# Doubled key tiles written by VectorE and turned a step later, and the gate's partial rows added instead of selected: one step of a hybrid attention layer

## The chip, the core and the metric

The kernel runs on one core of one Trainium2 chip. The metric is the time of one execution in microseconds (us), as the device measures it. Engines are named as in the profile: PE is TensorE, DVE is VectorE, ACT is ScalarE, POOL is GpSimd, SP is the sync engine, which only issues transfers here. ACT issues transfers too; "ACTq" and "SPq" rows are such issues.

## The reference

One layer of a diffusion backbone: 128 prompt tokens and 1024 latent tokens, width 1024. Cut to what matters:

```
shift, scale, gate = split(silu(cond) @ w_mod + b_mod, 3)      # cond: c (latent) and c_ctx (prompt)
h = rmsnorm(x, norm_gain) * (1 + scale) + shift
q_a, k_a, v_a, g_a, q_b, k_b, v_b, g_b = split(h @ w_in)       # 8 query heads and 2 key heads of 64 columns, per branch
q, k = rmsnorm per head, with gains; latent tokens: axial rotary positions
o_a = attention(q_a, all latent keys + 128 cached keys)        # prompt tokens: prompt keys only
o_b = attention(q_b, keys within 128 positions + cached keys, a learned sink per head)
y = x + gate * (concat(o_a * silu(g_a), o_b * silu(g_b)) @ w_out)
```

The outputs are y for prompt and latent tokens, and the prompt's keys and values. All in float32. The gate is one row of 1024 numbers per condition (two rows in all).

## The kernel before, in words

Tokens are worked in nine tiles of 128 (tile 0 is the prompt, tiles 1 to 8 are latent). To keep float32 accuracy at the fast matmul rate, each operand is split into a rounded high part (a cast, mostly on ACT) and a low part (the difference, on DVE or POOL), and a product is made of three: high x high, high x low, low x high. A projection of one tile is thus 24 products of 128x128x512 (lines 244 to 248).

**What sets the order.** The order is written by hand. `block` (line 265) runs one projection in two halves of 12 products; ahead of each half it calls `tick`, which moves a step counter on by one and runs what was entered in the `agenda` for that step with `later(n, f)`, in the order of entry. So a "step" is a half block of TensorE work, and side work is interleaved with it. At the end every engine is held to this program order; only waits between engines are left to the hardware. Buffers of one tag rotate: a tile that takes a buffer waits until the last reader of its predecessor is done.

The stages, in order: modulation and normalisation; gate projection of branch A; query projection of branch A, then of branch B (tiles 1 to 8, then 0); key and value projection (tile 0, then 1 to 8); gate projection of branch B; attention with the output projection.

**Queries** (`query`, line 614). For each tile: squares (ACT) and their sums (DVE), the power on POOL (`rsqrt_mean`, line 166), scaling and rotation (DVE), then at its seventh step the turn: four transposes by PE into a PSUM bank (line 650), the high part copied by ACT (653) and stored at once, the low part made by DVE a step later (658) and, with `later(1, ...)`, stored a step after that (`put`, two issues of 128 KB each on ACT's queue, line 663). `qo0` and `qo1` have two buffers each. The turns alternate between the two PSUM banks D and E (`bank_tr`, line 147), and so does everything else that calls `bank_tr`.

**The gate row** (`gate_rows`, line 597). During the queries of branch B, ahead of tile 4 and of tile 8, PE makes one half of the gate rows each time: eight products with 32 stationary columns, spread over the four column groups of the array, so that a PSUM bank holds four partial sums for each of the two conditions, at partitions 0-1, 32-33, 64-65 and 96-97. A step later ACT copies the bank to `grow` (604); three steps later `gate_sum` (591) adds the four partials by a float32 product with the selecting matrix `sel` (593), into a bank from `bank_tr`, and DVE adds the bias (594) and SP stores the row. Behind the second one come the splits of the key and value weights (231, 233), in the last query block.

**Keys** (`key`, line 783). The first three tiles (`AHEAD`), 0, 1 and 2, are projected while the query stage still drains; their key work is then entered at consecutive steps, the others' at every second step. For each tile: squares at its step 1; scaling and rotation on DVE at step 3; at step 4 (`final`, 813) DVE adds the two rotary products into `kf` (816; a copy for the prompt, 818) and in the same step ACT writes `k2`, each key head's 64 columns twice (`twice`, 749); at step 6 PE turns `k2` by four transposes into bank D or E (755), ACT casts the high parts (759 to 771), and a step later DVE makes the low parts (773), which lets the bank go. The cached keys (`put_keys(kc, ...)`, 831) go the same way from step 8. `kh`, the tag of `k2`, has two buffers.

Of the kernel before, what the change touches and what calls it, by code (L numbers as in the profile page):

```python
# [9 lines left out]
F32 = mybir.dt.float32  # L10
# [3 lines left out]
ALU = mybir.AluOpType  # L14
# [4 lines left out]
P = 128  # L19
# [32 lines left out]

WO_STEPS = ((0, 4, 4), (1, 5, 5), (2, 6), (3, 7), (4, 8, 6), (5, 9), (6, 11), (7, 12, 10), (8, 13), (9, 14), (10, 16))
TURN = 2
QUERY_AT = (0, 2, 3, 6)
PAD = 2
SECOND_FROM = 5
# [18 lines left out]
VC_AT = 6  # L76
ONES_AT = 14
KEY_AT = (1, 3, 4)
AHEAD = 3


# [24 lines left out]
def hybrid_step(ctx, tc, x_prompt, x_sample, cache_k_a, cache_v_a, cache_k_b, cache_v_b,  # L106
# [17 lines left out]
    def later(n, f):  # L124

        agenda.setdefault(now[0] + n, []).append(f)
# [20 lines left out]
    def bank_tr(name):  # L147
        turn["tr"] += 1
        return bank("DE"[turn["tr"] % 2], name)
# [159 lines left out]
    with tc.tile_pool(name="st", bufs=2, side="right") as st:  # L309
# [9 lines left out]
        def group_sum(out, eye):  # L319
            nc.vector.tensor_tensor(out, eye[:, 0:2], eye[:, 32:34], op=ALU.add)  # L320
            for a in (64, 96):
                nc.vector.tensor_tensor(out, out, eye[:, a : a + 2], op=ALU.add)

        wm = []

# [253 lines left out]
    with tc.tile_pool(name="qt", bufs=2, side="right") as qt:  # L579
# [4 lines left out]
        sil32 = qt.tile([P, KT, 32], F32, name="sil32g", bufs=1)  # L584
        nc.gpsimd.memset(sil32, 0.0)
        nc.vector.tensor_copy(sil32[:, :, 0:2], silc.rearrange("p (c k) -> p k c", c=2))
        sel = qt.tile([P, 2], F32, name="selg", bufs=1)
        group_sum(sel, ident_r.bitcast(F32))
        wg, bg = [], []

        def gate_sum(n, grow):
            pgs = bank_tr(f"pgs{n}")
            nc.tensor.matmul(pgs[0:2], sel, grow, start=True, stop=True)
            nc.vector.tensor_tensor(bg[n], pgs[0:2], bg[n], op=ALU.add)
            nc.sync.dma_start(gate_row[:, 512 * n : 512 * n + 512], bg[n])

        def gate_rows(n):
            pg = bank_mm(f"pgate{n}")
            for k in range(KT):
                a = 32 * (k % 4)  # L600
                nc.tensor.matmul(pg[a : a + 32], sil32[:, k, :], wg[2 * n + k // 4][:, k % 4, :],
                                 start=(k < 4), stop=(k >= 4), tile_position=(0, a))
            grow = qt.tile([P, 512], F32, tag="grow", name=f"grow{n}", bufs=1)
            later(1, lambda: nc.scalar.copy(grow, pg))
            later(3, lambda: gate_sum(n, grow))

        def load_wg(i):
            n, b = divmod(i, 2)
# [5 lines left out]
        def query(pq, m, t, tabs, n=1):  # L614

            nm = f"q{m}_{t}"
            pqv = pq.rearrange("p (h d) -> p h d", d=HD)
            v = {}

            def squares():  # L620
                sq = qt.tile([P, 8, HD], F32, tag="sq", name=f"sq{nm}")
                nc.scalar.activation(sq, pqv, AF.Square)  # L622
                ss = qt.tile([P, 8], F32, tag="ss", name=f"ss{nm}")
                nc.vector.tensor_reduce(ss, sq, axis=AX.X, op=ALU.add)
                v["r"] = rsqrt_mean(qt, ss, HD, 8, nm)

            def scale():
                qn = qt.tile([P, 8, HD], F32, tag="qn", name=f"qn{nm}")
                nc.vector.tensor_tensor(qn, pqv, v["r"].unsqueeze(2).to_broadcast([P, 8, HD]), op=ALU.mult)
                v["qn"] = qn  # L630
                if t:
                    v["rot"] = rope_products(qt, qn, 8, *tabs[m], t, nm)

            def rotated():

                qf = qt.tile([P, 4, 2, HD], F32, tag="qf", name=f"qf{nm}", bufs=3)
                out = qf.rearrange("p h g d -> p g h d")
                pair = lambda a: a.rearrange("p (g h) d -> p g h d", g=2)
                if t:
                    nc.vector.tensor_tensor(out, *(pair(a) for a in v["rot"]), op=ALU.add)  # L640
                else:
                    nc.vector.tensor_tensor(
                        out, pair(v["qn"]), gain4[:, 2 * m, :].unsqueeze(1).unsqueeze(1).to_broadcast([P, 2, 4, HD]),
                        op=ALU.mult)
                v["qf"] = qf

            def turned():
                ptq = bank_tr(f"pt{nm}")
                for h in range(4):
                    nc.tensor.transpose(ptq[:, P * h : P * h + P], v["qf"][:, h].rearrange("p g d -> p (g d)"),  # L650
                                        ident_r.bitcast(F32))
                qo = [qt.tile([P, 512], F32R, tag=f"qo{i}", name=f"qo{i}{nm}") for i in range(2)]
                nc.scalar.copy(qo[0], ptq)
                put(qo[0], 0)
                later(1, lambda: low(ptq, qo))

            def low(ptq, qo):
                nc.vector.tensor_tensor(qo[1], ptq, qo[0], op=ALU.subtract)
                later(1, lambda: put(qo[1], 1))

            def put(part, i):
                for g in range(2):
                    nc.scalar.dma_start(q_dram[t][m][64 * i : 64 * i + 64, 512 * g : 512 * g + 512],
                                       part[64 * g : 64 * g + 64].bitcast(F32))
# [62 lines left out]

    with tc.tile_pool(name="kt", bufs=2) as kt:
        W_GB.pools[WRAW : WRAW + 2] = [(kt, 2)] * 2
        sg_tile.append(lambda n: kt.tile([P, 512], F32, tag="kh", name=n))  # L730
        for b in range(0, 20, 4):
            later(4 + b // 2, lambda b=b: nc.gpsimd.tensor_scalar(
                v_hi[:, 0, b : b + 4, 1, :], gain4, 0.0, 1.0, op0=ALU.mult, op1=ALU.add))
# [9 lines left out]
        def put_keys(kf, blk, idx, nm, n):  # L743

            v = {}

            def twice():
                k2 = kt.tile([P, 4, 2, HD], F32, tag="kh", name=f"k2{nm}")
                nc.scalar.copy(k2, kf.unsqueeze(2).to_broadcast([P, 4, 2, HD]))
                v["k2"] = k2  # L750

            def turned():
                pt = bank_tr(f"pt{nm}")
                for i in range(4):
                    nc.tensor.transpose(pt[:, P * i : P * i + P], v["k2"][:, i].rearrange("p a d -> p (a d)"),
                                        ident_r.bitcast(F32))
                p4 = pt.rearrange("p (i n) -> p i n", n=P)
                if blk < 0:
                    nc.scalar.copy(khp, p4)
                    low = [(klp[0:64, 0:2], p4[0:64, 0:2], khp[0:64, 0:2]), (klp[:, 2:4], p4[:, 2:4], khp[:, 2:4])]  # L760
                else:
                    nc.scalar.copy(kha[:, :, blk, :], p4[:, 0:2])
                    low = [(kla[0:64, :, blk, :], p4[0:64, 0:2], kha[0:64, :, blk, :])]
                    if blk == 0:
                        for g in range(2):
                            four = p4[:, 2 + g].unsqueeze(1).to_broadcast([P, 4, P])
                            nc.scalar.copy(khb[:, g, 1::3, :], four)
                            low.append((klb[:, g, 1::3, :], four, khb[:, g, 1::3, :]))
# [4 lines left out]
                later(1, lambda: [nc.vector.tensor_tensor(*a, op=ALU.subtract) for a in low])  # L773

            for d, f in ((0, twice), (2, turned)):
                later(n + d, f)

        def put_values(src, t):
            j = 2 * t if t else 18
# [3 lines left out]
        def key(pk, t, idx):  # L783
# [5 lines left out]
            def squares():  # L789
# [4 lines left out]
                v["r"] = rsqrt_mean(kt, ss, HD, 4, nm)  # L794
                put_values(pkv[:, :, 1], t)
                if t == 0:
                    vn = kt.tile([P, 4, HD], F32, tag="kf", name="vn").rearrange("p (m g) d -> p m g d", m=2)
                    nc.scalar.copy(vn, pkv[:, :, 1])
                    for m in range(2):
                        nc.sync.dma_start((new_v_a, new_v_b)[m][0, 0], vn[:, m])  # L800
# [10 lines left out]
                    v["rot"] = rope_products(kt, kn, 4, *tabs, t, nm, 1)  # L811

            def final():
                kf = kt.tile([P, 4, HD], F32, tag="kf", name=f"kf{nm}")
                if t:
                    nc.vector.tensor_tensor(kf, *v["rot"], op=ALU.add)
                else:
                    nc.vector.tensor_copy(kf, v["kn"])
                    for m in range(2):
                        nc.sync.dma_start((new_k_a, new_k_b)[m][0, 0], kf[:, 2 * m : 2 * m + 2])  # L820
                put_keys(kf, t if t else -1, idx, nm, 0)
                tick_now()

            for d, f in zip(KEY_AT, (squares, scale, final)):
# [415 lines left out]
    def put(s, f):  # L1240
        due.setdefault(s, []).append(f)
# [109 lines left out]
```

## Time and profile before

| | |
|---|---|
| median of 3 runs | 716.38 us (716.08 to 716.65) |
| the profiled execution | 716.94 us |
| its span in the trace | 715.2 us |
| busy share of the span | TensorE 97%, VectorE 65%, ScalarE 58%, GpSimd 47% |
| granted TensorE clock, mean | 0.994 |

The span is what the trace covers from the first instruction to the last; the execution's own time is 1.7 us longer. A row of the timeline has the start, the duration, the engine, the line of the kernel, the operation, what it writes and from what, the shape, how many instructions were merged into the row, and in brackets how long the engine was idle before it and what ended that. Matmuls are pipelined: their recorded durations overlap, so what one costs is read from the distance of starts.

### The profile page before, as it was taken

How to read it: one execution, taken by the hardware profiler on the slowest of the kernel's cores; microseconds unless marked ns; L12 is line 12 of the kernel's file. 1: busy time of each engine (PE TensorE's matmuls, PEld its weight loads, DVE VectorE, ACT ScalarE, POOL GpSimd, SP SyncE). 2: the span in 40 equal slices, each digit the busy share in tenths (PEclk: the TensorE clock that was granted, in tenths of full speed). 3: DMA queues.
4: the chain of work that ended last, by engine and by line, in shares of the span. 5: the costliest groups of instructions: out<-in, count | busy, mean ns of one | idle time of the engine just before them, and what ended most of it. 6: DMA issues, size and time to landing. Idle time of an engine off the chain costs nothing. (4 is left out here: it accounts for less than half of the span.)

```text
span 715.2 us, 10633 instructions
## 1 busy us (share of the span) xinstructions
PE 694.4 (97%) x3512; PEld 559.1 (78%) x3512; DVE 463.8 (65%) x1016; ACT 416.4 (58%) x840; POOL 334.6 (47%) x356
## 2 busy tenths in 40 slices
PE   6999999999998999999999999999999999999987
PEld 4778988777686889976788888888888888887865
DVE  4767257866747864736867577567675775675662
ACT  5646411411414441178777877887788778877770
POOL 3647033232313320246757555755575557555651
PEclk9999999999999999999999999999999999999999
DMA  8962283358344026431222122122221221222323
GB/s 323 414 202 97 80 300 76 83 164 249 74 108 143 7 69 191 133 119 46 81 75 73 39 76 80 45 82 65 77 74 39 73 82 45 82 62 79 104 66 119
DMA packets 53304, 78.58 MB, mean 110 GB/s; under 512 B 6584, under 2 KB 25464, under 8 KB 52352
## 3 DMA queue, kind: packets, MB, share of 16 engines
q1 hardware_dynamic: 45072, 65.96, 28.0%
q10 hardware_dynamic: 8176, 11.94, 6.3%
q8 instruction: 28, 0.46, 0.3%
q14 instruction: 28, 0.23, 0.1%
HBM read 58.69 MB, written 19.18 MB: 109 GB/s over the span
## 5 line engine op out<-in xcount | busy, mean ns | idle before, releaser
L1136 POOL TENSOR_TENSOR pl<-pe,ph 128x512 fp32r<-128x512 f32 x130 | 167.7, 1292 | 145.4 <-DVE nm L947 67.6
L887 DVE TENSOR_REDUCE mx<-pmx 128x1 f32<-128x384 f32 x192 | 101.4, 552 | 60.2 <-PE pmx L886 58.9
L1128 ACT ACTIVATE pe<-st 128x512 f32<-128x512 f32 x146 | 86.9, 596 | 28.0 <-PE st L1126 27.0
L1132 ACT CAST ph<-pe 128x512 fp32r<-128x512 f32 x146 | 90.6, 620 | 4.8
L1146 PE MATMUL pv<-ph,v_hi 128*128 128x512 f32 x208 | 83.2, 400 | 2.2 <-DVE spare L1170 2.2
L1149 PE MATMUL pv<-pl,v_hi 128*128 128x512 f32 x208 | 82.5, 397 | 0.0
L171 POOL TENSOR_TENSOR rs_q<-ms_q,mhalf 128x8 f32<-128x8 f32 x18 | 34.8, 1931 | 82.2 <-DVE ms_q L169 82.2
L1217 PE MATMUL po<-wo,ogh 128*128 128x512 f32 x216 | 72.6, 395 | 0.2 <-DVE yt L1224 0.2
L947 DVE CUSTOM_DVE_ANT_0 sn<-sn,mask,nsink 128x512 f32<-128x512 f32 (+1 forms) x64 | 46.3, 724 | 38.4 <-PE sn L944 36.6
L886 PE MATMUL pmx<-kha,qt 128*128 128x384 f32 x192 | 60.9, 363 | 0.4 <-ACT pen L933 0.2
L1125 PE MATMUL st<-qt,kha 128*128 128x512 f32 x144 | 58.2, 404 | 1.5 <-ACT pe L1128 0.8
L1126 PE MATMUL st<-qb,kla 68*128 68x512 f32 x144 | 57.7, 401 | 1.1 <-DVE qb L906 1.1
L1148 PE MATMUL pv<-ph,v_lo 128*64 128x512 f32 x146 | 57.8, 396 | 0.0
L1149 PEld LDWEIGHTS pv<-pl,v_hi 128*128 128x128 f32 x208 | 39.3, 189 | 16.7 <-issue 0.4
L933 ACT ACTIVATE pen<-sn,nm 128x512 f32<-128x512 f32 (+2 forms) x72 | 45.1, 627 | 6.5 <-DVE nm L947 3.1
L1121 ACT CAST ph<-st 128x512 fp32r<-128x512 f32 x62 | 36.4, 588 | 19.9 <-PE st L1120 18.6
L1146 PEld LDWEIGHTS pv<-ph,v_hi 128*128 128x128 f32 x208 | 39.5, 190 | 10.7 <-ACT ogh L1182 2.4
L1217 PEld LDWEIGHTS po<-wo,ogh 128*128 128x128 f32 x216 | 39.9, 188 | 6.9 <-DVE yt L1224 0.6
L1122 DVE TENSOR_TENSOR pl<-st,ph 128x512 fp32r<-128x512 f32 x62 | 42.5, 686 | 2.1 <-ACT ph L1121 1.5
L1217 PE MATMUL po<-wo,ogl 128*128 128x512 f32 x108 | 42.5, 393 | 0.0
L622 ACT ACTIVATE sqq<-pq 128x512 f32<-128x512 f32 x18 | 10.8, 600 | 52.5 <-DMA qd<-qo0q 16.2
L886 PEld LDWEIGHTS pmx<-kha,qt 128*128 128x128 f32 x192 | 35.5, 190 | 6.3 <-DVE mx L887 1.4
(219 smaller groups left out, 1700.7 us busy)
## 6 DMA issues: line engine op xcount, KB each, us to landing
qt<-qd SPq DMA_DIRECT2D x36, 256.0 KB, 3.0
wm<-in_w_mod_ss_dram SPq DMA_DIRECT2D x7, 1024.0 KB, 10.0
qd<-qo0q ACTq DMA_DIRECT2D x36, 128.0 KB, 2.4
qd<-qo1q ACTq DMA_DIRECT2D x36, 128.0 KB, 2.4
sgl<-gd SPq DMA_DIRECT2D x36, 128.0 KB, 2.1
out_dram<-yt SPq DMA_DIRECT2D x17, 256.0 KB, 2.1
xn<-in_x_sample_dram SPq DMA_DIRECT2D x8, 512.0 KB, 6.1
wg<-in_w_mod_g_dram SPq DMA_DIRECT2D x4, 1024.0 KB, 8.4
```

Source lines behind the costliest of these rows:

```text
L886: nc.tensor.matmul(pm[:, 0:384], lhs, kha[:, g, 3 * b : 3 * b + 3, :], start=True, stop=True)
L887: nc.vector.tensor_reduce(mx[:, h, b : b + 1], pm[:, 0:384], axis=AX.X, op=ALU.max)
L947: nc.vector.tensor_tensor_reduce(s, s, mask[:, m0 : m0 + n], -1.0, nsink[:, 4 * g + h : 4 * g + h + 1], op0=ALU.add, op1=ALU.min, accum_ou ...
L1125: nc.tensor.matmul(s, kh, qtile[i], start=True, stop=False)
L1126: nc.tensor.matmul(s, kl, qbtile[i], start=False, stop=True)
L1128: nc.scalar.activation(pe, s, AF.Exp)
L1132: nc.scalar.copy(ph, pe)
L1136: nc.gpsimd.tensor_tensor(pl, pe, ph, op=ALU.subtract)
L1146: nc.tensor.matmul(pv, two, ph, start=(b == 0), stop=False)
L1148: nc.tensor.matmul(pv[0:64, :], vl, ph, start=False, stop=False)
L1149: nc.tensor.matmul(pv, two, pl, start=False, stop=last)
L1217: nc.tensor.matmul(po[n], a, wo_parts[KT * n + k][lo], start=(k == KS[0] and p == 0), stop=(k == KS[-1] and p == 2))
```

## The change

Three things.

1. Keys: DVE's `final` writes the doubled tile `k2` itself, by reading its operands with each head's columns repeated; the copy on ACT and `kf` are gone (the cached keys keep the copy on ACT). The turn comes three steps after `final` instead of two (`KEY_TURN`), and the tag `kh` has three buffers instead of two. The prompt's values `vn` get a buffer of their own.
2. The gate: `gate_sum` runs a step after `gate_rows` instead of three, and adds the four partial rows to the bias row straight from the PSUM bank, by four DVE adds of 2x512. The copy to `grow`, the matrix `sel` with its three small adds, and the selecting product are gone.
3. Queries: the low part is stored two steps after it is made instead of one (`PUT_LOW`).

```
+PUT_LOW = 2
+KEY_TURN = 3
+KEYS = 3
...
-        sel = qt.tile([P, 2], F32, name="selg", bufs=1)
-        group_sum(sel, ident_r.bitcast(F32))
...
-        def gate_sum(n, grow):
-            pgs = bank_tr(f"pgs{n}")
-            nc.tensor.matmul(pgs[0:2], sel, grow, start=True, stop=True)
-            nc.vector.tensor_tensor(bg[n], pgs[0:2], bg[n], op=ALU.add)
+        def gate_sum(n, pg):
+            for a in range(0, P, 32):
+                nc.vector.tensor_tensor(bg[n], pg[a : a + 2], bg[n], op=ALU.add)
             nc.sync.dma_start(gate_row[:, 512 * n : 512 * n + 512], bg[n])
...
-            grow = qt.tile([P, 512], F32, tag="grow", name=f"grow{n}", bufs=1)
-            later(1, lambda: nc.scalar.copy(grow, pg))
-            later(3, lambda: gate_sum(n, grow))
+            later(1, lambda: gate_sum(n, pg))
...
-                later(1, lambda: put(qo[1], 1))
+                later(PUT_LOW, lambda: put(qo[1], 1))
...
-        sg_tile.append(lambda n: kt.tile([P, 512], F32, tag="kh", name=n))
+        sg_tile.append(lambda n: kt.tile([P, 512], F32, tag="kh", name=n, bufs=KEYS))
...
-            def twice():
-                k2 = kt.tile([P, 4, 2, HD], F32, tag="kh", name=f"k2{nm}")
-                nc.scalar.copy(k2, kf.unsqueeze(2).to_broadcast([P, 4, 2, HD]))
-                v["k2"] = k2
...
-            for d, f in ((0, twice), (2, turned)):
-                later(n + d, f)
+            later(n + KEY_TURN, turned)
...
-                    vn = kt.tile([P, 4, HD], F32, tag="kf", name="vn").rearrange("p (m g) d -> p m g d", m=2)
+                    vn = kt.tile([P, 4, HD], F32, name="vn", bufs=1).rearrange("p (m g) d -> p m g d", m=2)
...
+        def two(a):
+
+            return a.unsqueeze(2).to_broadcast([P, 4, 2, HD])
...
             def final():
-                kf = kt.tile([P, 4, HD], F32, tag="kf", name=f"kf{nm}")
+                k2 = kt.tile([P, 4, 2, HD], F32, tag="kh", name=f"k2{nm}", bufs=KEYS)
                 if t:
-                    nc.vector.tensor_tensor(kf, *v["rot"], op=ALU.add)
+                    nc.vector.tensor_tensor(k2, *(two(a) for a in v["rot"]), op=ALU.add)
                 else:
-                    nc.vector.tensor_copy(kf, v["kn"])
+                    nc.vector.tensor_copy(k2, two(v["kn"]))
...
-        put_keys(kc, 0, 0, "c", CACHE_AT)
+        def cached():
+            k2 = kt.tile([P, 4, 2, HD], F32, tag="kh", name="k2c", bufs=KEYS)
+            nc.scalar.copy(k2, two(kc))
+            put_keys(k2, 0, 0, "c", 0)
+            tick_now()
+
+        later(CACHE_AT, cached)
```

More of the change, by code (lines that the diff above doesn't have):

```diff
@@ L317, in hybrid_step @@
         st.tile([P, 16], F32, name="pad3", bufs=1)
[L319 to L322, printed above, removed]
         wm = []
@@ L741, in hybrid_step, with put_keys @@
             nc.sync.dma_start(tabs[-1], src)
-        def put_keys(kf, blk, idx, nm, n):
-            v = {}
-            def twice():
-                k2 = kt.tile([P, 4, 2, HD], F32, tag="kh", name=f"k2{nm}")
-                nc.scalar.copy(k2, kf.unsqueeze(2).to_broadcast([P, 4, 2, HD]))
-                v["k2"] = k2
+        def two(a):
+            return a.unsqueeze(2).to_broadcast([P, 4, 2, HD])
+        def put_keys(k2, blk, idx, nm, n):
             def turned():
@@ L754, in turned @@
                 for i in range(4):
-                    nc.tensor.transpose(pt[:, P * i : P * i + P], v["k2"][:, i].rearrange("p a d -> p (a d)"),
+                    nc.tensor.transpose(pt[:, P * i : P * i + P], k2[:, i].rearrange("p a d -> p (a d)"),
                                         ident_r.bitcast(F32))
@@ L813, in final @@
             def final():
-                kf = kt.tile([P, 4, HD], F32, tag="kf", name=f"kf{nm}")
+                k2 = kt.tile([P, 4, 2, HD], F32, tag="kh", name=f"k2{nm}", bufs=KEYS)
                 if t:
-                    nc.vector.tensor_tensor(kf, *v["rot"], op=ALU.add)
+                    nc.vector.tensor_tensor(k2, *(two(a) for a in v["rot"]), op=ALU.add)
                 else:
-                    nc.vector.tensor_copy(kf, v["kn"])
+                    nc.vector.tensor_copy(k2, two(v["kn"]))
                     for m in range(2):
-                        nc.sync.dma_start((new_k_a, new_k_b)[m][0, 0], kf[:, 2 * m : 2 * m + 2])
-                put_keys(kf, t if t else -1, idx, nm, 0)
+                        nc.sync.dma_start((new_k_a, new_k_b)[m][0, 0], k2[:, 2 * m : 2 * m + 2, 0])
+                put_keys(k2, t if t else -1, idx, nm, 0)
                 tick_now()
```

## The prediction

> **What bounds the kernel now.** I read the page's first table, then the matrix engine's waits over the whole run, the busy time by stretches of 20 us, and last the timeline around each place that the change touches.
>
> ```profile
> PE 694.4 (97%) x3512; PEld 559.1 (78%) x3512; DVE 463.8 (65%) x1016; ACT 416.4 (58%) x840; POOL 334.6 (47%) x356
> ```
>
> TensorE works 97% of the span. So time is won in two ways only: take work off TensorE, or take away one of the few places where it waits. Of these the change can reach three:
>
> ```profile
> PE ptk L755 <- DVE klp L773: 1.4, 1, 1.4
> PE ptk L755 <- ACT k2k L749: 1.1, 1, 1.1
> PE ptq L650 <- DVE qo1q L658: 0.5, 1, 0.5
> ```
>
> The first two are key turns, the third is a query turn. Whether another engine can take more work is read by stretches (columns: TensorE, its weight loads, VectorE, ScalarE, GpSimd, clock, DMA share, GB/s):
>
> ```profile
> 160.00:180.00 20.00, 19.94 (x93) 15.17 (x95) 13.34 (x27) 3.56 (x6) 6.36 (x4) 1.00 0.79 237
> 180.00:200.00 20.00, 19.50 (x97) 14.18 (x90) 15.44 (x29) 8.19 (x15) 5.23 (x3) 1.00 0.38 90
> 220.00:240.00 20.00, 17.50 (x86) 14.01 (x85) 17.94 (x72) 9.71 (x25) 7.14 (x10) 1.00 0.26 80
> ```
>
> VectorE has room where the gate rows are summed (160 to 200), and almost none where the first keys are made: 17.94 of 20 us, while TensorE loses 2.5. There VectorE is the bound, and there the change gives it more.
>
> **The gate's sum.** TensorE's cost of the selecting product is read from starts, with it and without it:
>
> ```profile
> 160.45 0.60 PE L650 MATMUL ptq<-ident_r,qfq 128*128 128x128 f32 x4
> 161.11 1.02 PE L593 MATMUL pgs<-grow,selg 128*2 128x512 f32 x2
> 162.06 0.50 PE L246 MATMUL pq<-whiqb,h 128*128 128x512 f32 x1
> ...
> 167.64 0.60 PE L650 MATMUL ptq<-ident_r,qfq 128*128 128x128 f32 x4
> 167.99 0.48 PE L246 MATMUL pq<-whiqb,h 128*128 128x512 f32 x1
> ...
> 187.43 0.60 PE L650 MATMUL ptq<-ident_r,qfq 128*128 128x128 f32 x4
> 189.02 0.50 PE L246 MATMUL pq<-whiqb,h 128*128 128x512 f32 x1
> ```
>
> From the turn to the next projection product it is 0.35 us without the selecting product, 1.61 and 1.59 with it. So the two cost 1.26 + 1.24 = 2.50 us, with no wait in them: **-2.50**, the surest term. The copy into grow and the three tiny adds that make sel go from engines with room: nothing.
>
> The selecting product also takes a turn of the two banks D and E that the query turns alternate on. At the second gate it comes between the turns of tiles 5 and 6 and takes D, so tile 6 falls on E, the bank of tile 5, and waits until VectorE has made tile 5's low part:
>
> ```profile
> 194.37 0.39 PE L248 MATMUL pq<-whiqb,h 128*128 128x512 f32 x1
> 195.22 0.63 PE L650 MATMUL ptq<-ident_r,qfq 128*128 128x128 f32 x4 [0.46 <-DVE qo1q L658]
> ```
>
> Products start 0.23 apart, so tile 6's turn could start at 194.60 and starts at 195.22: 0.62. Without the selecting product it falls on D, which tile 4 left three steps before: **-0.62**.
>
> In exchange VectorE makes four adds of 2x512 where it made one, two steps earlier. The price of one is the page's own:
>
> ```profile
> L594 DVE TENSOR_TENSOR bg<-pgs,bg x2: 671/676/681, 163.9 to 191.0; 2x512 f32<-2x512 f32 x2
> ...
> 183.96 1.20 ACTq L663 DMA_DIRECT2D qd<-qo1q  x2
> 185.84 0.69 DVE L624 TENSOR_REDUCE ssq<-sqq 128x8 f32<-128x512 f32 x1 [2.40 <-ACT sqq L622]
> 188.86 0.69 DVE L629 TENSOR_TENSOR qnq<-pq,rs_q 128x512 f32<-128x512 f32 x1 [0.93 <-POOL rs_q L171]
> 194.99 3.69 DVE L233 TENSOR_TENSOR wlokv<-rawkv,whikv 128x512 fp32r<-128x512 f32 x6
> 197.30 0.39 PE L247 MATMUL pk<-wlokv,h 128*128 128x512 f32 x1
> ```
>
> Four cost 2.70 and stand behind ssq. The second gate is the tight one, because the key weights' low parts (L233) follow. Moving the store of a query's low part a step later (PUT_LOW) takes its two issues, 1.2 us, out from in front of the squares on ScalarE, so ssq starts 1.2 earlier, out of its idle 2.40. Behind the adds, the 0.93 that VectorE waited for rs is gone, and the old add, 0.68, too: 2.70 - 1.20 - 0.93 - 0.68 is -0.1, so VectorE reaches its splits about as early as before. TensorE though comes 1.24 + 0.62 = 1.86 earlier. Split 2 ends at 194.99 + 0.69 = 195.68, less 0.1; the product that needs it is then due at 197.30 - 1.86 = 195.44. A new wait of some 0.15 to 0.2: **+0.2**. If ScalarE doesn't give the 1.2, it is about 1.3; if VectorE gains more, nothing. At the first gate no splits follow, and the turns of these queries come three steps later: nothing.
>
> Elsewhere PUT_LOW moves only stores. Queued behind them on ScalarE are squares and high parts, and a later store holds back the low part that reuses its buffer, two tiles on, two steps after it; a step of 12 products is 2.7 us and a store lands in 2.4 us, so no new wait:
>
> ```profile
> qd<-qo1q ACTq DMA_DIRECT2D x36, 128.0 KB, 2.4
> ```
> At the end of the queries the order on ScalarE is unchanged. Price: nothing.
>
> **The keys.** The doubled copy leaves ScalarE (nine of them; no gain by itself), VectorE's add grows from 256 columns to 512, and the turn comes at step 7 of a key instead of 6. TensorE and VectorE now:
>
> ```profile
> 221.35 0.39 PE L248 MATMUL pk<-whikv,h 128*128 128x512 f32 x1
> 222.81 0.66 PE L755 MATMUL ptk<-ident_r,k2k 128*128 128x128 f32 x4 [1.06 <-ACT k2k L749]
> 226.07 0.60 PE L755 MATMUL ptk<-ident_r,k2k 128*128 128x128 f32 x4
> 229.03 0.39 PE L248 MATMUL pk<-whikv,h 128*128 128x512 f32 x1
> 230.85 0.63 PE L755 MATMUL ptk<-ident_r,k2k 128*128 128x128 f32 x4 [1.43 <-DVE klp L773]
> 234.06 0.60 PE L755 MATMUL ptc<-ident_r,k2c 128*128 128x128 f32 x4
> ...
> 224.45 0.41 DVE L816 TENSOR_TENSOR kfk<-ra_k,rb_k 128x256 f32<-128x256 f32 x1
> 224.78 0.84 DVE L807 SCALAR_TENSOR_TENSOR knk<-pk,rs_k,gain 128x64 f32<-128x64 f32 x4
> 229.97 0.74 DVE L773 TENSOR_TENSOR klp<-ptk,khp 64x256 fp32r<-64x256 f32 x2
> 230.63 0.40 DVE L793 TENSOR_REDUCE ssk<-sqk 128x4 f32<-128x256 f32 x1
> 231.15 0.42 DVE L816 TENSOR_TENSOR kfk<-ra_k,rb_k 128x256 f32<-128x256 f32 x1
> ```
>
> By starts, the first turn (the prompt's key) could begin at 221.35 + 0.23 = 221.58 and begins at 222.81, 1.23 late. The third could begin at 229.26 and begins at 230.85, 1.59 late, as bank D still holds the prompt's turn until VectorE's klp is done at 230.71. Together 2.82.
>
> With the change TensorE reaches the prompt's turn one half block (12 products, 2.72) later, at 224.30; its doubled key is then there (about 222.3), so the first wait is gone. A step with a turn is 3.2 long (230.85 to 234.06), so the third turn is due at 230.70. It still waits for klp, and that moves too: klp is now issued a step later, behind ssk and ms (0.52 from 230.63 to 231.15) and behind the third latent key's add. That add takes 0.60 by pitch: a 128x512 add is 0.69 long (L629 above) and the next starts 0.1 before its end. The two keys before it pay 0.60 instead of 0.33 each, +0.54, and the prompt's doubled copy about 0.13. So klp ends at 230.71 + 0.52 + 0.60 + 0.54 + 0.13 = 232.50, and the third turn starts 0.14 behind that, as now, at 232.64 instead of 230.70: a wait of 1.94 in place of 2.82, **-0.88**. The cached key's turn is due 3.2 later, at 235.85; its bank is free at about 235.2 (klp's end, about 0.4 of value splits, 1.6 of the next key's scaling and rotation, 0.7 of two low parts): no wait, and from there on keys come every second step and nothing is late.
>
> What this takes for nothing: with three buffers alive at once, the cached key's copy on ScalarE waits for the prompt's turn (224.96); behind it are only khp and the squares, which klp does not miss. The third latent key's add likewise waits for the first latent key's turn (done by 228.2), but VectorE comes to it only at about 231.5. The last key's turn falls into the next step, so its two casts go ahead of the third gate piece's SiLU on ScalarE; the store of that piece, and the query loads behind it on SP's queue, come about 0.7 later:
>
> ```profile
> 271.94 1.76 SPq L866 DMA_DIRECT2D qt<-qd  x4
> ...
> 276.59 0.34 PE L886 MATMUL pmx<-kha,qt 128*128 128x384 f32 x1
> ...
> qt<-qd SPq DMA_DIRECT2D x4, 256.0 KB, 3.3
> ```
>
> The first product that reads a loaded query starts 4.65 behind the first load, which lands in 3.3: 0.6 to spare.
>
> One rule speaks against the doubled add. GpSimd's power (rs_k) took 1.04 beside a 256-column add and 1.99 beside a long VectorE write:
>
> ```profile
> 237.15 1.04 POOL L171 TENSOR_TENSOR rs_k<-ms_k,mhalf 128x4 f32<-128x4 f32 x1 [4.33 <-DVE ms_k L169]
> 242.21 1.99 POOL L171 TENSOR_TENSOR rs_k<-ms_k,mhalf 128x4 f32<-128x4 f32 x1 [3.64 <-DVE ms_k L169]
> 242.79 1.35 DVE L736 TENSOR_SCALAR kla<-ident_r 4x2304 fp32r<-4x2304 f32 x1
> ```
>
> The Trainium skill, "SBUF — State Buffer", section "SBUF: two separate sides", says that VectorE with two SBUF inputs and a GpSimd operation share one port pair, held for a whole instruction. By it the power would end up to 0.27 later per key, and the wait of 1.94 would be 2.2. The 1.99 agrees, the 1.04 hardly does; the sum goes without it.
>
> **The sum**: -2.50 - 0.62 + 0.20 - 0.88 = -3.80. The profiled execution took 716.94 (span 715.2), so it would take 713.14; it lies 0.56 above the median of the runs, 716.38, which becomes **712.6**. Behind the keys TensorE sets the pace, and the gain is carried to the end.
>
> **Rivals.**
> Both key waits vanish: if VectorE comes 1.9 us earlier against TensorE, klp is in time. That is -2.50 - 0.62 - 2.82 = -5.9, 710.4. For it speaks that ScalarE's queue loses the copies that waited for VectorE; against it, that VectorE has hardly an idle moment from 219 to 231. 0.15.
>
> The key stage gains nothing and the gate's adds hold up the weight splits: a key wait of 3.0 (+0.2), +1.3 at the splits: -2.50 - 0.62 + 1.3 + 0.2 = -1.6, 714.8. For it: VectorE's 17.94 of 20. 0.18, a third of it with a little more lost at the query loads and so within 0.2% of no change.
>
> Slower: VectorE takes over as the bound from the second half of the queries to the keys' end, and each added microsecond of it lands on TensorE: 2 x 3 x 0.68 + 9 x 0.27 = 6.5, less 2.50 and 0.62: +3.4, 719.8. It decides where VectorE's busy time plus what is added passes the stretch: 13.34 + 2.0 and 15.44 + 2.0 don't, 17.94 + 1.3 = 19.2 comes near. 0.06.
>
> The change frees TensorE but a later stage, waiting for a load, gives it back; the query loads above, with 0.6 to spare, are the nearest, and could return about half a microsecond, not four. It gives 716.4. 0.06.
>
> **The numbers.** The forecast has 0.55 (-3 to -5). The range goes from the first rival, 710.4, to just past the second, 715.0. A measurement here can tell about 0.2%, 1.43 us, so faster means under 714.95: 0.55 + 0.15 + 0.12 = 0.82. Within: 0.06 + 0.06 = 0.12. Slower: 0.06.
>
> **What would show it.** In the changed profile L593's products are gone and the turn-to-projection time is 0.35 everywhere; the query turn after the second gate waits for nothing; TensorE's wait for the doubled key's writer is gone and one wait for klp of 1.6 to 2.2 us is left at the third key turn; the wlokv wait is under 0.5. If the klp wait is gone, or over 3, the key step is wrong; if VectorE's adds show up in front of a waiting projection product, the gate step is. The forecast falls if TensorE's total wait after 240 us grows by over a microsecond.

## The result and the profile after

The changed kernel takes 711.56 us in the median of 6 runs (711.44 to 712.55) against 716.23 of the kernel before (715.53 to 716.65, 6 runs beside it): a ratio of 0.9938, 95% interval 0.9925 to 0.9951, 4.67 us. The forecast was 712.6, range 710.4 to 715.0. The profiled execution took 711.52, its span is 709.6. The page's first table, TensorE's waits and two stretches of 20 us (columns as in the prediction):

```profile
PE 691.6 (97%) x3508; PEld 558.5 (79%) x3508; DVE 469.3 (66%) x1019; ACT 409.9 (58%) x829; POOL 334.2 (47%) x356
```

```profile
PE ptk L745 <- DVE klp L763: 1.2, 1, 1.2
```

```profile
180.00:200.00 20.00, 19.98 (x94) 16.18 (x94) 17.05 (x31) 8.29 (x15) 4.07 (x3) 1.00 0.37 93
220.00:240.00 20.00, 18.75 (x93) 15.25 (x92) 19.53 (x68) 6.16 (x17) 6.20 (x7) 1.00 0.25 73
```

Of the three waits that the prediction started from, one is left in the list, the one for klp. VectorE took the work: 17.05 of 20 us in the second gate's stretch (15.44 before) and 19.53 at the first keys (17.94 before), while TensorE lost 1.25 there instead of 2.50. (The stretches are fixed in time, and the changed kernel is 2 to 5 us further on in its work there, so the columns show the load, not the same instructions.) VectorE's idle time, which made the edits cheap at the gates, is used up at the keys.

**Where the time went, by starts.** TensorE behind the second gate, in the changed kernel:

```profile
185.20 0.39 PE L251 MATMUL pq<-whiqb,h 128*128 128x512 f32 x1
185.43 0.60 PE L643 MATMUL ptq<-ident_r,qfq 128*128 128x128 f32 x4
185.78 0.48 PE L249 MATMUL pq<-whiqb,h 128*128 128x512 f32 x1
...
191.13 0.39 PE L251 MATMUL pq<-whiqb,h 128*128 128x512 f32 x1
191.36 0.60 PE L643 MATMUL ptq<-ident_r,qfq 128*128 128x128 f32 x4
...
192.74 0.39 PE L250 MATMUL pk<-wlokv,h 128*128 128x512 f32 x1
...
193.61 0.50 PE L250 MATMUL pk<-wlokv,h 128*128 128x512 f32 x1
```

From the turn to the next projection product it is 0.35 where it was 1.59, and tile 6's turn follows the last product by 0.23 where it stood 0.85 behind it. The two wlokv products are 0.87 apart; three pitches of 0.23 are 0.69, so 0.18 is the new wait for the split.

The keys, first on TensorE, then on VectorE:

```profile
220.88 0.60 PE L745 MATMUL ptk<-ident_r,k2k 128*128 128x128 f32 x4
...
227.08 0.39 PE L251 MATMUL pk<-whikv,h 128*128 128x512 f32 x1
228.72 0.63 PE L745 MATMUL ptk<-ident_r,k2k 128*128 128x128 f32 x4 [1.25 <-DVE klp L763]
...
231.96 0.60 PE L745 MATMUL ptc<-ident_r,k2c 128*128 128x128 f32 x4
```

```profile
215.63 0.29 DVE L718 TENSOR_TENSOR v_lo<-pk,v_hi 128x128 fp32r<-128x128 f32 x1 [1.69 <-ACT vn L787]
...
218.25 0.42 DVE L807 COPY k2k<-knk 128x512 f32<-128x512 f32 x1
...
227.23 0.68 DVE L805 TENSOR_TENSOR k2k<-ra_k,rb_k 128x512 f32<-128x512 f32 x1
227.83 0.74 DVE L763 TENSOR_TENSOR klp<-ptk,khp 64x256 fp32r<-64x256 f32 x2
```

The first wait is gone; the third turn could start at 227.08 + 0.23 = 227.31 and starts at 228.72, 0.14 behind klp (the low part of the prompt's key): 1.41 late, in place of 2.82 in two waits before.

One gain stands where the forecast had none. In the kernel before, TensorE waited once for a query weight's low part (the first row is the product that it follows by 0.23 elsewhere):

```profile
135.99 0.40 PE L246 MATMUL pq<-whiqb,h 128*128 128x512 f32 x1
...
136.67 0.50 PE L247 MATMUL pq<-wloqb,h 128*128 128x512 f32 x1 [0.28 <-DVE wloqb L233]
```

That is 0.68 instead of 0.23, so 0.45, and in the changed kernel these products run 0.23 apart. At the last two query turns 0.12 is lost (0.91 from the turns to the next product, 0.79 before). The sum over the places: -0.45 - 2.50 - 0.62 + 0.18 + 0.12 - 1.41 = -4.68, against -4.67 between the medians. That the two agree to a hundredth is luck: the interval leaves 0.9 us on either side. The two profiled executions differ by more, 716.94 - 711.52 = 5.42: 0.2 of it lies ahead of the change's reach, and the rest at the start of the attention, where the granted clock was 0.91 (300 to 320 us) in the profile of before and 1.00 in this one. That drop is no property of the kernel; the last section says how often it came.

### The profile page after: what moved, and what is told of

The parts are those of the page before. It is cut to its first block, busy times and chain, and to the rows that moved or that the text cites. A ratio compares the mean times of both kernels' runs of the same rounds, so it can differ in the third digit from the quotient of the medians.

```text
span 709.6 us, 10604 instructions
## 1 busy us (share of the span) xinstructions
PE 691.6 (97%) x3508; PEld 558.5 (79%) x3508; DVE 469.3 (66%) x1019; ACT 409.9 (58%) x829; POOL 334.2 (47%) x356
## 5 line engine op out<-in xcount | busy, mean ns | idle before, releaser
L646 ACT CAST qo0q<-ptq 128x512 fp32r<-128x512 f32 x18 | 10.6, 586 | 60.7 <-PE ptq L643 55.8
```

## The experiments

Twelve runs, in three sets: ten further kernels, one of them twice, and the changed kernel once more. Each set ran on one chip with the kernel before beside it, and the ratios are to that. "By starts" means a distance of starts on TensorE less the undisturbed distance.

| kernel | us, median | ratio, 95% interval |
|---|---|---|
| gate_alone | 715.22 | 0.9982 (0.9973 to 0.9992) |
| store_alone | 714.61 | 0.9974 (0.9964 to 0.9984) |
| keys_alone | 715.30 | 0.9983 (0.9972 to 0.9995) |
| store_back | 713.31 | 0.9958 (0.9942 to 0.9974) |
| turn2 | 712.56 | 0.9936 (0.9922 to 0.9949) |
| act_copy | 711.66 | 0.9924 (0.9911 to 0.9938) |
| bank_turn | 713.00 | 0.9944 (0.9930 to 0.9957) |
| low_now | 712.04 | 0.9927 (0.9914 to 0.9941) |
| after_again | 711.63 | 0.9929 (0.9915 to 0.9942) |
| combo | 713.20 | 0.9953 (0.9936 to 0.9970) |
| gate_store | 713.20 | 0.9955 (0.9942 to 0.9968) |
| store_back_2 | 713.26 (one run) | none |

The kernel before took 716.36 beside the first four, 717.25 beside the next four, 716.38 beside the last four. Intervals of some 0.2 to 0.3% do not separate most neighbours in this table; what separates them is TensorE's waits, read in each trace.

**Theory**: the terms of the last section, each at its own place, with the store's move worth 0.45 at the query weights and the 1.2 us of room for the key weights. **Rivals**: the store is worth nothing (as the prediction had it); the query turn's wait is not a matter of banks; the doubled write on VectorE is what shortens the key wait.

### One part at a time

gate_alone: the change's part 2 alone, on the kernel before.

```
-            later(3, lambda: gate_sum(n, grow))
+            later(1, lambda: gate_sum(n, pg))
```

> Only the gate's part of the change. Theory (each part acts where its wait is): the two selecting products go, -2.50, tile 6's query turn no longer waits, -0.62, but the squares on ScalarE still stand behind the store, so VectorE comes about 1.2 us late to the key weights' splits and TensorE waits about 1.4 us for one of them: -1.7 us against the kernel before, with a wait for wlokv of 1.2 to 1.5. Rival (the store's later place has nothing to do with the gate, VectorE has room): a wait under 0.3 there and -2.9 us.

It gained 1.14 by the medians. The query turn's wait was gone. The wait for wlokv was there twice, 0.47 + 0.91 = 1.38 by starts. And the wait for wloqb had grown from 0.45 to 0.92, which neither theory had. The trace says why: on ScalarE two issues of a store took 2.62 together there (2.09 in the kernel before), and the squares stand behind them. ScalarE and TensorE of gate_alone:

```profile
125.34 2.62 ACTq L653 DMA_DIRECT2D qd<-qo1q  x2
128.01 0.60 ACT L612 ACTIVATE sqq<-pq 128x512 f32<-128x512 f32 x1 [3.90 <-issue]
```

```profile
137.79 0.50 PE L247 MATMUL pq<-wloqb,h 128*128 128x512 f32 x1 [0.76 <-DVE wloqb L233]
```

By starts -2.50 - 0.62 + 1.38 + 0.47 = -1.27, near the 1.14.

store_alone: the change's part 3 alone.

```
-                later(1, lambda: put(qo[1], 1))
+                later(PUT_LOW, lambda: put(qo[1], 1))
```

> Only the later store of a query's low part. Theory: the squares come 1.2 us earlier on ScalarE and with them VectorE, so the wait for wloqb (0.45 by starts) goes, and the query turn of tile 6 finds its bank free (0.62): -1.1 us against the kernel before, both waits gone from the list. Rival, the prediction's own word that the later store costs and gives nothing: 0, both waits as they were.

It gained 1.75 by the medians. The waits for wloqb and for the query turn's bank were both gone, the key waits as before. ScalarE of the kernel before and of store_alone, at the same store:

```profile
124.74 2.09 ACTq L663 DMA_DIRECT2D qd<-qo1q  x2
126.88 0.60 ACT L622 ACTIVATE sqq<-pq 128x512 f32<-128x512 f32 x1 [3.37 <-issue]
```

```profile
124.73 0.60 ACT L623 ACTIVATE sqq<-pq 128x512 f32<-128x512 f32 x1 [1.18 <-issue]
124.81 2.09 ACTq L664 DMA_DIRECT2D qd<-qo1q  x2
```

The pair of issues is as long in both, but the squares now stand ahead of it and come 2.15 earlier. So "nothing" is refuted. By starts 0.45 + 0.62 is 1.07; the 0.7 beyond that is not accounted for by its waits.

gate_store: both of these, keys as before (the two edits above together).

> The gate's adds and the later store, keys as before. Theory: the store's lead of 1.2 on ScalarE is what keeps the key weights' splits in time for the gate's adds, so together they bring -2.50 - 0.62 - 0.45 + 0.2 = -3.4 (the two alone brought -1.1 and -1.2 by their times), with the wait for wlokv under 0.3, and the two key waits stay at 2.7 to 3.0. Rival (the store is worth nothing, as the prediction had it): wlokv waits 1.4 as with the gate alone, and the sum is -1.7 to -2.2.

It gained 3.18. No wait for wlokv or wloqb is listed (by starts there is the 0.18 at wlokv that the changed kernel has too), and the key waits are near those of the kernel before, 1.05 + 1.62 = 2.67 by starts:

```profile
PE ptk L746 <- DVE klp L764: 1.5, 1, 1.5
PE ptk L746 <- ACT k2k L740: 0.9, 1, 0.9
```

That is near the theory's -3.4 and beyond the rival's -1.7 to -2.2; the wlokv wait, 0.18 where gate_alone had 1.38, decides it: the store pays for the room that the gate's adds need.

store_back and store_back_2: the changed kernel with the store back at one step.

```
-PUT_LOW = 2
+PUT_LOW = 1
```

> The changed kernel with the store put back to one step. Theory: the wloqb wait returns (0.45) and VectorE is 1.2 us later at the key weights' splits: +1.6 us against the changed kernel, -3.1 against the kernel before. Rival (the store does not matter): as the changed kernel, -4.7.

> The changed kernel with the store a step earlier again, a second profile. Theory of the clock: behind the gap of 2.5 us at the third key turn the granted clock falls to about 0.7 for some 4 us and the products come 0.43 apart, as in the first profile. Rival: that was a chance of that execution; the products behind the gap come 0.23 apart and the clock stays at 1.00, with the gap itself the same.

Without the store's move the kernel takes 713.31, against 711.56 and 711.63 with it (in other sets; the ratios are 0.9958 against 0.9938 and 0.9929). In both profiles wlokv is waited for twice:

```profile
PE pk L250 <- DVE wlokv L236: 1.0, 2, 0.7
```

By starts it is 0.46 + 0.90, about the 1.3 that the prediction gave for the case without the lead. The wait for wloqb is back as well, smaller than the 0.45 expected: 0.29 and 0.38 by starts. Beyond that the two profiles of this one kernel differ: the key wait was 2.36 in the first and 1.29 in the second. That is taken up below.

keys_alone: the change's part 1 alone (the hunks of `put_keys`, `final` and `kh`).

> Only the keys' part. Theory: the two waits of 2.82 us by starts become one for klp at the third turn, 1.2 to 1.6: -1.4 us against the kernel before. The prediction's figure: a wait of 1.94, -0.9. Rival (VectorE is the bound in this stage and gets 0.26 us more per key): no gain, 0.

It gained 1.06. One key wait is left, 1.55 by starts; the waits at wloqb and at the query turn are as in the kernel before. The three parts alone gained 1.14 + 1.75 + 1.06 = 3.95, the whole change 4.67. So each part acts where it was made, but two of them meet: the gate and the store both remove the query turn's wait, and the store removes the 1.38 at wlokv that the gate's adds cause.

### The key turn

turn2: the changed kernel, the turn back at two steps.

```
-KEY_TURN = 3
+KEY_TURN = 2
```

> The changed kernel with the turn two steps after the add again (three buffers and VectorE's doubled add kept). Theory: what won time in the keys is the later turn; without it the first turn waits about 0.6 us for the doubled key and the third about 2.3 for klp, 2.9 in place of 1.41: +1.5 us against the changed kernel. Rival (the gain comes from taking the copy off ScalarE): waits of 1.4 or less in all, no difference.

Both waits were back:

```profile
PE ptk L745 <- DVE klp L763: 2.2, 1, 2.2
PE ptk L745 <- DVE k2k L807: 0.5, 1, 0.5
```

By starts 2.35 + 0.63 = 2.98, against 1.41. So what shortens the waits is the later turn, not VectorE's doubling. The times do not show it: turn2's ratio is 0.9936, against 0.9938 and 0.9929 for the changed kernel, where the 1.5 us that were expected would make it about 0.995 to 0.996. The profile does show the loss where it arises: beside the profile after, TensorE is about 1.6 us later behind the keys than ahead of them. It regains some 0.5 in small steps behind 460 us; why the median shows nothing of the rest stays open.

act_copy: the changed kernel with the doubling back on ScalarE, turn and buffers as changed.

```
-                    nc.vector.tensor_tensor(k2, *(two(a) for a in v["rot"]), op=ALU.add)
+                    nc.vector.tensor_tensor(kf, *v["rot"], op=ALU.add)
...
+                nc.scalar.copy(k2, two(kf))
```

> The changed kernel with the doubling put back on ScalarE (VectorE adds 256 columns, ScalarE copies them twice in the same step), with the turn still three steps later and three buffers. Theory: VectorE is the bound here and its doubled write costs about 0.9 us ahead of klp; with it gone the klp wait falls from 1.41 to about 0.5: -0.9 us against the changed kernel. Rival (ScalarE's copies hold back khp and with it klp, as in the kernel before): the wait stays or grows, 0 to +1.

```profile
227.78 0.63 PE L745 MATMUL ptk<-ident_r,k2k 128*128 128x128 f32 x4 [0.73 <-DVE klp L763]
```

The wait is 0.88 by starts: 0.53 shorter without the doubled write, so that write costs the key stage half a microsecond. The theory had 0.9. The ratio, 0.9924, does not separate it from the changed kernel.

low_now: the changed kernel, with the low parts of the prompt's and of the next turned key made in the step of the turn.

```
-                later(1, lambda: [nc.vector.tensor_tensor(*a, op=ALU.subtract) for a in low])
+                lows = lambda: [nc.vector.tensor_tensor(*a, op=ALU.subtract) for a in low]
+                if idx in (1, 2):
+                    lows()
+                else:
+                    later(1, lows)
```

> The changed kernel, with the low parts of the first two keys issued in the step of their turn, so that klp stands ahead of the third latent key's scaling, the sums and its add on VectorE. Theory (the last wait in the key stage is klp's place in VectorE's order, not VectorE's total work): bank D is free at about 226 and TensorE reaches the third turn at 227.3: the wait goes, -1.4 us against the changed kernel, -6.1 against the kernel before. Rival (VectorE's total work is the bound): the wait moves to a later turn, 0 to -0.4.

The key wait was gone: the third turn follows the last product, which starts at 226.91, by 0.23. TensorE waited instead in the next stage, for the gate weights' low parts:

```profile
227.14 0.60 PE L745 MATMUL ptk<-ident_r,k2k 128*128 128x128 f32 x4
...
250.53 0.50 PE L264 MATMUL pg<-h,wlogb 128*128 128x512 f32 x1 [0.70 <-POOL wlogb L236]
...
252.34 0.50 PE L264 MATMUL pg<-h,wlogb 128*128 128x512 f32 x1 [0.16 <-POOL wlogb L236]
...
254.98 0.39 PE L264 MATMUL pg<-h,wlogb 128*128 128x512 f32 x1
```

By starts 0.86 + 0.30 of the 1.41 went there, and a little more at the products behind each wait: the product of the last row starts at 254.96 in the changed kernel, so TensorE has nothing left of the gain. Nor does the median, 712.04, show any. What the run does show is that the order of VectorE's work made the key wait: the same work, in another order, left none there.

combo: an attempt at a better kernel; only the prompt's low part early, the doubling on ScalarE, two late splits taken from GpSimd.

```
-            eng = eng or (nc.gpsimd if self.tag in POOL_LO and k % 2 else nc.vector)
+            eng = eng or (nc.gpsimd if self.tag in POOL_LO and k % 2 and k < 5 else nc.vector)
...
+                if blk < 0:
+                    lows()
```

> The changed kernel with the doubling back on ScalarE, the prompt's low part made in the step of its turn, and the gate weights' low parts from piece 6 on left to VectorE. Theory: the one key wait of 1.41 goes wholly; TensorE then reaches the second half of the gate 1.4 us earlier, where an earlier trial waited 0.70 + 0.16 for low parts that GpSimd made in 1.29 each and VectorE makes in 0.69, so these go too or shrink to 0.3; 1.0 to 1.4 us under the changed kernel. Rival: the gate weights' loads, which wait for raw buffers, set the pace there whatever engine makes the low parts; then a wait of about 0.9 stands and the gain is 0.5 or less.

It missed what was expected of it (1.0 to 1.4 under the changed kernel): 713.20, against 711.63 beside it. The wait at the third turn was gone, and the fourth waited for the other bank:

```profile
PE ptc L745 <- DVE klb L763: 1.9, 1, 1.9
```

By starts 2.01, which is 0.6 more than the wait that went. The low part that was made later now came last: the order of VectorE's work chooses which bank is late. The three edits were made together, so they can't be told apart. The profiled execution, 714.20, lost a further 1.6 at the start of the attention, where the granted clock was 0.83 (300 to 320 us).

bank_turn: the changed kernel with one turn of the banks skipped behind each gate sum, as the selecting product did.

```
             later(1, lambda: gate_sum(n, pg))
+            later(3, lambda: turn.update(tr=turn["tr"] + 1))
```

> The changed kernel, with one turn of the banks D and E left out behind each gate sum, as the selecting product's bank took one; no instruction is added. Theory (the query turn of tile 6 waited for its bank, not for its data): the turn falls on tile 5's bank again and waits about 1.6 us for tile 5's low part, while the later wait of 0.18 for wlokv goes: +1.4 us against the changed kernel. Rival (the wait was VectorE's general lateness): no difference.

```profile
193.19 0.63 PE L644 MATMUL ptq<-ident_r,qfq 128*128 128x128 f32 x4 [1.58 <-DVE qo1q L652]
```

The wait is back, 1.73 by starts; it is longer than the 0.62 of the kernel before, since TensorE now comes to this turn earlier. It came from the banks' turn, not from the data: nothing else was changed. The ratio, 0.9944, points the same way, but its interval (0.9930 to 0.9957) holds the changed kernel's 0.9938.

### The changed kernel once more

after_again is the changed kernel itself, for the comparison in the third set.

> The changed kernel itself, once more, so that the other kernels of this set stand beside it on the same chip. Theory (gate products -2.50, query turn's bank -0.62, first wait for a query weight's split gone -0.45, key waits 2.82 to 1.41, 0.3 given back at the splits and at the end of the queries: -4.7 in all): about 4.7 us under the kernel before, 0.9935, with one key wait of 1.2 to 1.4. If the 4.7 was in part a chance of one profile, another key wait.

Its median is the same, 711.63. Its profiled execution, though, took 715.56, and shows what had looked like a peculiarity of store_back. ScalarE's queue at the last query tile but one, first in the profile after, then in this one:

```profile
205.27 0.61 ACTq L656 DMA_DIRECT2D qd<-qo0q  x1
```

```profile
205.12 1.69 ACTq L656 DMA_DIRECT2D qd<-qo0q  x1
```

One issue took 1.08 longer. Behind it on ScalarE stand the last tile's cast and stores, and the squares of the first key; VectorE's last query low part waits for one of these stores to land. VectorE of the two, in the same order:

```profile
211.03 0.69 DVE L651 TENSOR_TENSOR qo1q<-ptq,qo0q 128x512 fp32r<-128x512 f32 x1 [4.56 <-DMA qd<-qo1q]
```

```profile
211.98 0.69 DVE L651 TENSOR_TENSOR qo1q<-ptq,qo0q 128x512 fp32r<-128x512 f32 x1 [5.65 <-DMA qd<-qo1q]
...
228.77 0.74 DVE L763 TENSOR_TENSOR klp<-ptk,khp 64x256 fp32r<-64x256 f32 x2
```

klp is 0.94 later, TensorE is 0.15 earlier, and the key wait is 1.09 longer:

```profile
226.93 0.39 PE L251 MATMUL pk<-whikv,h 128*128 128x512 f32 x1
229.66 0.63 PE L745 MATMUL ptk<-ident_r,k2k 128*128 128x128 f32 x4 [2.34 <-DVE klp L763]
...
231.17 0.63 PE L249 MATMUL pk<-whikv,h 128*128 128x512 f32 x1
231.60 0.63 PE L250 MATMUL pk<-wlokv,h 128*128 128x512 f32 x1
...
234.46 0.60 PE L745 MATMUL ptc<-ident_r,k2c 128*128 128x128 f32 x4
```

Behind the wait the products stand 0.43 apart instead of 0.23. The granted clock (third column from the right) in single microseconds, same execution; it was 1.00 in the microsecond before and in the one behind:

```profile
230.00:231.00 1.00, 1.00 (x6) 0.86 (x5) 0.97 (x5) 0.68 (x3) 0.10 (x1) 0.68 0.00 0
231.00:232.00 1.00, 1.00 (x3) 0.73 (x3) 1.00 (x5) 0.52 (x2) 0.00 (x0) 0.50 0.00 0
232.00:233.00 1.00, 1.00 (x4) 0.78 (x3) 0.97 (x4) 0.00 (x0) 0.13 (x1) 0.50 0.00 0
233.00:234.00 1.00, 1.00 (x5) 0.76 (x4) 1.00 (x4) 0.00 (x0) 1.00 (x1) 0.61 0.00 0
```

From the third to the fourth turn it is 4.80 instead of 3.24 (231.96 - 228.72 in the profile after): 1.56 lost to the clock, 1.09 to the wait. So one long issue cost 2.65. The other 1.4 of the 4.04 between the two executions lies later: a wait of 0.64 for `mx` and a granted clock of 0.91 from 300 to 320 us, though the gaps ahead of it are as long in the profile after, where the clock stayed at 1.00. store_back shows the same chain (its pair of issues took 2.19, its key wait 2.36, clock 0.72 from 230 to 235), and store_back_2, with the pair at 1.10, a wait of 1.29 and the clock at 1.00.

## Why the prediction was right, and where it was not

**The selecting products, -2.50**: right to the hundredth, 0.35 at both gates (159.70 to 160.06 and 185.43 to 185.78).

**The bank of tile 6's turn, -0.62**: right, and bank_turn brought the wait back with nothing but the bank.

**The splits, +0.2**: 0.18. VectorE's four adds took 2.85 where 2.70 was worked out:

```profile
182.54 0.69 DVE L617 TENSOR_REDUCE ssq<-sqq 128x8 f32<-128x512 f32 x1 [2.73 <-ACT sqq L615]
...
183.46 2.85 DVE L589 TENSOR_TENSOR bg<-pgate,bg 2x512 f32<-2x512 f32 x4
```

The condition that the prediction attached, ScalarE's lead of 1.2, is what carries it: without the lead store_back waited 1.36.

**The store elsewhere, "nothing"**: this step failed. It looked at the store as something that could only come late (a held buffer), and took what its two issues hold up on ScalarE, the squares of the next tile, for nothing outside the second gate. At the query weights that cost TensorE 0.45, because VectorE reached the splits at 133.52 there; in store_alone it reaches them at 132.10. The same reading had been made at the second gate, and was not carried to the others. How large the wait is goes with one long issue in that pair: where the store comes early, this issue took 1.00, 1.38, 1.44, 1.45 and 1.97 (store_back, store_back_2, before, keys_alone, gate_alone), and the wait by starts was 0.29, 0.38, 0.45, 0.45 and 0.92.

**The keys, -0.88**: the mechanism was right, the size was not: -1.41. The first wait vanished and the one for klp stayed, listed with 1.2 where the prediction named 1.6 to 2.2 as its sign. The terms inside were right (the three adds at 0.60 by pitch, the copy at 0.42 for 0.29, ssk and ms ahead of klp). But VectorE's way from the first value split to klp's end grew from 11.51 (219.20 to 230.71) to 12.94 (215.63 to 228.57), 1.43 and not 1.79, since small waits between its operations went into the added work: it no longer waits 0.17 for the power, and the first ra_k took 0.53 for 0.62. The other 0.17 is TensorE, later against VectorE by that much. The other profile of the same kernel had 2.50; the 1.94 of the forecast lies between the two, so its size is also a matter of the execution.

**The rule against the doubled add** ("SBUF — State Buffer", "SBUF: two separate sides", in the Trainium skill): the power beside a 512-column add took 1.31, against 1.04 beside the 256-column one, just the 0.27 that the rule gave.

```profile
227.47 1.31 POOL L174 TENSOR_TENSOR rs_k<-ms_k,mhalf 128x4 f32<-128x4 f32 x1 [2.06 <-DVE ms_k L172]
```

It cost nothing, since klp is queued ahead of what reads the power. By that rule the wait would have been 2.2; it was 1.41. The prediction took the 1.04 for a case that hardly agrees, and it does agree: before, the add beside that power ended at 237.32 and the power at 238.19; after, at 227.91 and 228.78. In both the power ends 0.87 behind the add.

**What was taken for nothing behind the keys**: in the profile after no group of TensorE's waits behind 240 us is more than 0.3 longer (1.1 in two waits for `pe`, 0.8 in one before), and the query loads were in time. In after_again one wait of 0.64 came up there.

**The rivals.** That both key waits vanish needed VectorE 1.9 earlier; it had 19.53 of 20 us to do. That VectorE becomes the bound from the queries on did not happen: there TensorE waits 0.18. At the first keys VectorE has hardly an idle moment, and had none to spare before the change; yet even there the wait comes from the order of its work, since low_now has none. That the gain is given back by a load did not happen.

**The sum.** The forecast was -3.80, the places came to -4.68. The 0.88 between them is 0.53 at the keys, 0.45 at the query weights and 0.02 at the splits, less 0.12 lost at the last query turns.

What stays open: why store_alone gained 0.7 more than its waits; why turn2's time does not show its waits; what makes single issues a microsecond longer (the last section says what goes with them); and whether the higher ones among the changed kernel's thirteen runs (712.55, 712.95, 713.79; nine lie from 711.42 to 711.79) have the cause that the one at 715.56 shows, since they have no profile. Earlier or fewer stores at the end of the queries, the head of the chain to klp, were not tried.

## To carry to other kernels

Transfers issued from a computing engine's queue are work of that engine: look at what stands behind each issue, and put the computation that others wait for ahead of it. Where two banks take turns, a product that is removed also shifts every later turn, so follow the parity to its end. And where one engine is full for the length of a stage, reordering its work can take a wait away from it, but look where it turns up: here at another bank (combo) or in the next stage, behind another engine (low_now). The event that starts the stage, here a store at the end of the one before, is the other place to look; moving that was not tried.

## What the runs showed of the hardware

An issue of a 128 KB store on ScalarE's queue took 0.45 to 0.61 us mostly, and what stood behind it started after it (the squares at 126.88, behind a pair from 124.74 to 126.83). But in each of the fourteen profiles one issue at 123.9 to 125.4 us took 1.00 to 1.97, and in three of them one more at 205 to 207 us took 1.22 to 1.71 (low_now, after_again, store_back). These 17 long issues have something in common in the traces: within 0.45 us of the start of each, a packet of 16 KB starts on a queue that the page lists as one for instructions.

```profile
q8 instruction: 28, 0.46, 0.3%
```

In the other eleven profiles such a packet starts at 205 to 209 us too and no issue is long. So no long issue comes without such a packet; that the packet makes the issue long is not shown.

TensorE's clock halved behind key waits of 2.34 and 2.36 us (distances of starts 2.73 and 2.75), for 3.41 us (230.37 to 233.78 in after_again, 232.18 to 235.59 in store_back); behind key waits of 2.19 (turn2), 1.85 (combo) and 1.25 it stayed at 1.00. The length of the wait is not all that counts. In each of the fourteen profiles all steps of the granted clock lie on one grid of 3.41 us, at another place in each execution: in after_again 230.37, 233.78, 312.29 and 315.70, where 312.29 - 230.37 = 81.92 is 24 times 3.413. Both waits that halved the clock lay whole between two marks of the grid, while a mark at 225.49 cut the 2.19 of turn2 into 0.46 and 1.73. The 1.85 of combo lay whole between two marks too, and did not halve it. And at the start of the attention, where no wait of TensorE is longer than 0.80, the clock halved in seven of the fourteen profiles (before, store_alone, gate_store, act_copy, bank_turn, combo and after_again) and stayed at 1.00 in the other seven, with waits of the same lengths.

The Trainium skill, "TensorE: Matmul & The Clock Gate", Part 1, puts the step to half clock at an idle window of about 3.4 us that runs freely. The grid and the length at half clock agree with that; but here less than a window of idle time was enough. How much idle time within one window it takes, these runs don't settle.

An add of 2x512 out of PSUM took VectorE 0.71 by pitch (2.85 for four), and a difference of 128x512 out of PSUM 0.69 (`qo1q` above): two partitions cost as much as 128.
